# SwiGLU in quarters: 18 instead of 14 hidden tiles by seven products, two of the seven accumulated onto banks that were already read

## The chip, the cores and the metric

The kernel runs on one core of a Trainium2 chip. The metric is device time in microseconds (us), from the launch of the program to its end. The engines are named as the profile names them: PE is the tensor engine (PEld its weight loads), DVE the vector engine, ACT the scalar engine, POOL GpSimd, and SP the engine whose queue issues most of the DMAs. The profile sees the span from the first to the last instruction.

## What is computed

One decoder layer over 528 tokens (16 meta tokens and 512 main ones), with 1024 features: a half-weighted SwiGLU block, a mixing layer (attention and retention), and a second half-weighted SwiGLU block. The change touches the two SwiGLU blocks only:

```python
def swiglu(x, w_in, w_out):
    a, b = jnp.split(x @ w_in, 2, axis=-1)
    return (jax.nn.silu(a) * b) @ w_out

h = h + 0.5 * swiglu(rmsnorm(h, norm_ffn1), w_ffn1_in, w_ffn1_out)
...
h = h + 0.5 * swiglu(rmsnorm(h, norm_ffn2), w_ffn2_in, w_ffn2_out)
```

There are 2816 hidden features, that is 22 hidden tiles of 128 features, each with an `a` half and a `b` half. Everything is float32.

## The kernel before, in words

**Layout and precision.** Features lie on partitions, tokens on the free axis. Every dense product splits both float32 operands into a high and a low float32r part and takes three passes (high by high, high by low, low by high). ACT makes the high part by a copy, DVE the low part by a subtraction; the pair is the helper `split` (lines 104 to 106), so that each split is one ACT and one DVE instruction.

**A hidden tile as a whole.** `aj` and `bj` in the order `SEQ` (line 36) are the two halves of hidden tile j: eight chunks of 128 input features, three passes, each matmul over all tokens (two matmuls of 272 and 256 tokens in the first block, one of 512 in the second, which leaves the meta tokens out). `gated` then makes silu(a) times b.

**A hidden tile by seven products.** `ej` and `lj` compute both halves of tile j with seven products of quarters where a plain calculation has eight (a Strassen-like scheme). The quarters are the output halves, the contraction halves (chunks 0 to 3 and 4 to 7) and the token halves (t1, t2; 264 tokens each in the first block, 256 in the second). A product (`prod`) is four chunks by three passes, 12 matmuls. `early` (lines 387 to 404) has the first four products and `late` (lines 406 to 419) the last three. DVE adds and subtracts their results between the products. The scheme needs sums of the weights' quarters, made by `wsums` on DVE (lines 184 to 193: four additions of 512 columns per tile), and sums of the input's quarters, made by `usums` (lines 328 to 347), called at `u0` to `u3` for one pair of input chunks each; they are called `xa` and `xb` and can only be made once the norm's factor R is there. In the trace the products' tiles are `fq` in the first block and `sq` in the second, the whole halves `fpa`, `fpb`, `spa`, `spb`, and the output tiles (`pi`) `fpo`, `spo`.

**PSUM.** The products have four one-bank buffers (tag `pq`), the whole halves and output tiles two buffers of two banks (tag `ps`).

**Output tiles.** The hidden tiles are grouped in four parts of 6, 5, 6 and 5 (`PJ`). `pi` multiplies one of eight output tiles with part i, and DVE adds it onto the residual.

**The weights' stream.** SP loads 1 MB weight tiles ahead. A weight piece of up to 1024 columns is split into `wh` and `wl`, which have four buffers each. `weights()` (lines 219 to 224) hands out the next piece and first emits the splits of the pieces up to two further on. For a tile by seven products the pieces are `("A0","S1")`, `("A2","S0")`, `("A1","S2")` and `("A3",)`, where A0 to A3 are the tile's quarters as loaded (A2 is overwritten by a difference) and S0 to S2 sums of quarters; each name is a split of 512 columns of its own.

**Order.** PE's order is the one written in the code (`manual_schedule`). On DVE and ACT a scheduler places the instructions when the kernel is built: what is emitted earlier goes first among what is ready, and at run time each engine takes its instructions in the order so fixed. `gated` of tiles 0 to 3 is raised by 30 places.

Of the kernel before, what the change touches and what calls it, by code (L numbers as in the profile page):

```python
"""Hybrid decoder layer (FoX attention + retention between two half SwiGLU blocks), one core.

Everything is kept feature-major: features on partitions, tokens on the free axis.  The zero rows
that the reference puts before the meta tokens are masked everywhere, so the token axis here has the
16 meta tokens followed by the 512 main ones.  Dense products split both float32 operands exactly
into a float32r high and low part and take three passes (hh, hl, lh).  Most hidden tiles of the
SwiGLU blocks are computed by seven products of quarters (output halves x contraction halves x token
halves) instead of eight; the sums of quarters are float32 sums, split exactly like the other operands.
"""
# [11 lines left out]
ALU = mybir.AluOpType  # L21
# [10 lines left out]
# The order of a SwiGLU's work on the tensor engine, one token a piece or two of weights:  n0, n1: the  # L32
# first two hidden tiles; aj, bj: the halves of hidden tile j; ej, lj: a hidden tile by seven products of
# quarters, its first four and its last three; pi: the next output tile of the i-th part of the hidden
# tiles.  ui marks where the i-th chunk's sums of quarters are made.
SEQ = """n0 n1 a2 u0 b2 u1 a3 u2 b3 u3 a4 b4 e5 l5
          e6 p0 p0 l6 p0 e7 p0 p0 l7 p0 p0 p0
          e8 l8 e9 a10 l9 b10 e11 p1 l11 p1 p1 e12 p1 l12 p1 e13 p1 l13 p1 p1
          e14 a15 l14 b15 e16 l16 e17 p2 p2 l17 p2 e18 p2 p2 l18 p2 p2 p2
          e19 l19 e20 a21 l20 b21 p3 p3 p3 p3 p3 p3 p3 p3""".split()  # L40
# [12 lines left out]
# Tensor engine work (in units of its time) put between the steps of the attention: FOXFILL scales it,  # L53
# CREDIT is the number of the gates' tiles that go with a pair of heads.
# [10 lines left out]
def layer(tc, order, hT, wf1i, wf1o, wf2i, wf2o, wmix, wsq, vecs, cs, rmask, rvec, cmask, outT):  # L65
# [3 lines left out]
    with ExitStack() as es:  # L69
# [24 lines left out]
        def po_(a):  # L94
            """Where token 0 lies in a two-bank PSUM tile: no matmul's tokens cross the banks."""
            return PO if a == 0 else PM
# [15 lines left out]
        def weave(main, fill):  # L112
            """Emit main; what it yields is the tensor engine time to fill before it goes on."""
            have = 0.0
            for need in main:
                have -= need
                while have < 0:
                    got = next(fill, None)
                    if got is None:
                        have = 0.0  # L120
                        break
                    have += got

        # ---------------------------------------------------------------- the weights' stream
# [10 lines left out]
        def feed_ffn(seq, w_in, w_out):  # L135
            at_, nxt = {}, [0] * len(PJ)
            for tok in seq:
# [12 lines left out]
                if c in "nae":  # L150
# [3 lines left out]
                        "e": [("A0", "S1"), ("A2", "S0")], "l": [("A1", "S2"), ("A3",)]}[c]  # L154
                pieces.extend((at_[j], x, 1024) for x in cuts)
# [28 lines left out]
        def wsums(i):  # L184
            """Sums of a weight tile's quarters A11, A12, A21, A22: S1, S2, S4, and S3 in A21's place."""
# [9 lines left out]
        def ready(n):  # L195
            while at["p"] < min(n, len(pieces)):
# [11 lines left out]
                if i < 2:  # L208
                    for x in (0, 512):
                        split(wh[:, x:x + 512], wl[:, x:x + 512], raw[li][:, c + x:c + x + 512])  # L210
                        gained(2 * i + x // 512, gn1, u, 0, "n1")
                elif loads[li][2] == "S":
                    for x, src in enumerate(c):
                        src = (raw, sums)[src[0] == "S"][li][:, 512 * int(src[1]):512 * int(src[1]) + 512]
                        split(wh[:, 512 * x:512 * x + 512], wl[:, 512 * x:512 * x + 512], src)
                else:
                    split(wh[:, :w], wl[:, :w], raw[li][:, c:c + w])
# [8 lines left out]
        # ---------------------------------------------------------------- constants and first loads  # L226
# [41 lines left out]
        # ---------------------------------------------------------------- helpers  # L268
        def mm3(outs, w, x, nk, first=True, last=True):
            """outs = w^T x over nk chunks of 128, three float32r passes; outs: (psum, first token, end)."""  # L270
# [14 lines left out]
        def mm3s(out, w, x, start=True, stop=True):  # L285
            for i, (p, q) in enumerate(((w[0], x[0]), (w[0], x[1]), (w[1], x[0]))):
                nc.tensor.matmul(out, p, q, start=start and i == 0, stop=stop and i == 2)  # L287

        def gained(k, g, u, a, name):
            """u = h * gain, split into high and low parts."""  # L290
# [14 lines left out]
        def rstd(acc, R, outs, a, name, er=None):  # L305
            """R = rsqrt(mean square + eps) of every token, on all partitions."""
# [16 lines left out]
        # ---------------------------------------------------------------- SwiGLU  # L323
# [4 lines left out]
        def usums(c, gain, a, xs, name):  # L328
            """Sums of the quarters of h * gain * R (chunk halves x token halves), split: they pair
            tokens, which have one scale only when they are normed."""  # L330
# [18 lines left out]
        def ffn(seq, u, gain, a, pst, pq, norm, done, name):  # L349
# [5 lines left out]
            def prod(out, w, off, x, k0, ts, first, last):  # L355
                """out (+)= w^T x over four chunks: one of the seven products of quarters."""
                for k in range(4):
                    c = slice(off + 128 * k, off + 128 * k + 128)
                    mm3s(out, [z[:, c] for z in w], [z[k0 + k][:, ts] for z in x], first and k == 0, last and k == 3)
# [27 lines left out]
            def early(j):  # L387
                """The four products that the others' sums start from, and these sums."""
                b = [pq(f"{name}q{j}_{x}")[:, :nh] for x in range(4)]
                cu = ttile(f"{name}cu{j}")[:, :2 * nh]  # L390
                d = ttile(f"{name}d{j}")[:, :nh]
                bv = ttile(f"{name}b{j}")[:, :2 * nh]
                w = weights()
                prod(b[0], w, 0, u, 0, t1, True, True)
                nc.vector.tensor_tensor(cu[:, x1], b[0], R[:, t1], ALU.mult)
                prod(b[1], w, 512, xa, 0, x2, True, True)
                nc.vector.tensor_tensor(cu[:, x2], cu[:, x1], b[1], ALU.add)
                w = weights()
                prod(b[2], w, 512, xa, 0, x1, True, True)
                nc.vector.tensor_tensor(d, cu[:, x2], b[2], ALU.add)  # L400
                prod(b[3], w, 0, xb, 0, x1, True, True)
                nc.vector.tensor_tensor(bv[:, x1], cu[:, x2], b[3], ALU.add)
                nc.vector.tensor_tensor(bv[:, x2], d, b[3], ALU.add)
                return b, cu, d, bv

            def late(j, b, cu, d, bv):
                w = weights()
                prod(b[0], w, 0, u, 4, t1, True, True)
                prod(b[2], w, 512, u, 4, t2, True, True)
                prod(b[3], weights(), 0, xb, 0, x2, True, True)  # L410
                sv = ttile(f"{name}s{j}")[:, :2 * nh]
                nc.vector.tensor_tensor(sv[:, x1], b[0], R[:, t1], ALU.mult)
                nc.vector.tensor_tensor(sv[:, x2], b[2], R[:, t2], ALU.mult)
                nc.vector.tensor_tensor(bv[:, x1], bv[:, x1], b[3], ALU.add)
                nc.vector.tensor_tensor(sv[:, x1], sv[:, x1], cu[:, x1], ALU.add)
                nc.vector.tensor_tensor(sv[:, x2], sv[:, x2], d, ALU.add)
                nc.scalar.activation(sv, sv, AF.Silu)
                nc.vector.tensor_tensor(sv, sv, bv, ALU.mult)
# [3 lines left out]
            for tok in seq:  # L422
                c, j = tok[0], int(tok[1:])
                if tok == "n0":
# [3 lines left out]
                    # set aside: the tiles' banks are needed before R is there  # L428
# [25 lines left out]
                else:  # L454
# [5 lines left out]
                    # the last one in halves: the first is stored while the second is computed  # L460
# [6 lines left out]
        # ---------------------------------------------------------------- first SwiGLU  # L467
# [35 lines left out]
        # ---------------------------------------------------------------- mixing  # L503
# [8 lines left out]
        with tc.tile_pool(name="psM", bufs=1, space=PSUM, reuse_waits="tile") as pM:  # L512
# [9 lines left out]
            def proj(what, a, one=False):  # L522
                """One 128-wide tile of the combined projection of the unscaled u."""
# [9 lines left out]
            # ---- forget gate: running sum of the negated log sigmoid, every head a row in DRAM  # L533
# [36 lines left out]
            # ---- retention's projections  # L570
# [34 lines left out]
            # ---- forgetting attention  # L605
            y32 = [None] * KC
            last = {}
            with tc.tile_pool(name="fx", bufs=1, reuse_waits="tile") as fx:
# [11 lines left out]
                def qknorm(v, gain, a, name):  # L620
                    """Per-head RMS norm of a projected tile (64 features to a head), split: for each head of
                    a pair its keys' high and low parts one above the other, its queries' high part
                    twice, so that one pass of 128 rows carries both products with it."""
# [32 lines left out]
                def late(gen, fill):  # L656
                    """Run gen with its waits filled from fill; what is emitted is yielded on."""
# [12 lines left out]
                def values(p, v):  # L670
# [7 lines left out]
                    # a head's high and low parts side by side: one pass gives both products  # L678
# [542 lines left out]
```

## Time and profile before

| what | value |
|---|---|
| time, three runs | 1394.41, 1394.80 and 1395.88 us, median 1394.8 us |
| span of the profiled execution | 1392.1 us (its own time outside the span is not listed) |
| median less that span | 2.7 us |
| mean granted clock of PE | 0.999 of full speed |
| busy share PE, PEld, DVE, ACT | 99%, 89%, 72%, 48% |
| mean DMA traffic | 100 GB/s, 139.41 MB |

A share of busy time is a mean over stages with different limits; whether an engine sets the pace in one stage is read from that stage. Matmuls are pipelined: the listed duration of one is longer than the distance from its start to the start of the next. The same holds to a lesser degree on DVE and ACT, so that what an instruction costs in a full queue is the distance from start to start.

### The profile page before, as it was taken

Reading aid. Unit: us, or ns where it says so; the run is one execution under the profiler, and the core shown is the slowest. Engines: PE = TensorE matmul, PEld = TensorE weight load, DVE = VectorE, ACT = ScalarE, POOL = GpSimd, SP = SyncE. Lnnn points to the kernel's source line nnn. Section 1 sums busy time; section 2 is a strip of 40 time slices with the busy share of each in tenths; the row PEclk is TensorE's granted clock in tenths of the full one; section 3 lists DMA queues with packets and bytes.
Section 4 is the critical chain, followed back from the end, with each engine's and each line's share of the span. In section 5 each row is a group of like instructions: output and inputs, shape, how many; then the busy total and the mean of one; then the engine's idle time right before and its main releaser. Section 6 shows DMA issues by size and latency. Waiting matters only on the chain.

```text
span 1392.1 us, 22206 instructions
## 1 busy us (share of the span) xinstructions
PE 1376.5 (99%) x8871; PEld 1232.8 (89%) x8871; DVE 1007.9 (72%) x1948; ACT 666.7 (48%) x1131; POOL 52.6 (4%) x80
## 2 busy tenths in 40 slices
PE   8999999999999999999999999999999999999999
PEld 7999999999988788877878998888888889899897
DVE  7977877866687676677755866754666977788773
ACT  7433333333567577666754534453435433344331
POOL 0000000000013000010000000000100000000000
PEclk9999999999999999999999999999999999999999
DMA  7123222221513222222222112433521232223302
GB/s 276 46 106 110 79 101 106 84 103 64 201 61 109 92 84 71 90 92 84 92 84 91 61 61 71 139 124 136 191 108 57 80 127 82 99 93 121 109 21 97
DMA packets 27814, 139.41 MB, mean 100 GB/s; under 512 B 3632, under 2 KB 4016, under 8 KB 16576
## 3 DMA queue, kind: packets, MB, share of 16 engines
q1 hardware_dynamic: 24336, 127.31, 25.5%
q0 software_dynamic: 3232, 10.65, 2.6%
q8 instruction: 70, 1.15, 0.3%
q14 instruction: 32, 0.26, 0.1%
q10 hardware_dynamic: 144, 0.04, 0.0%
HBM read 129.56 MB, written 8.42 MB: 99 GB/s over the span
## 4 chain that ended last, share of the span: by engine, by line
PE 96%; DVE 2%; ACT 1%; DMA 0%; issue 0%; SPq 0%; DVEq 0%; ACTq 0%
PE fq L287 10%; PE sq L287 10%; PE fpo L277 9%; PE spo L277 9%; PE pg L277 6%; PE prv L277 3%; PE fpb L277 3%; PE pq L277 3%; PE fpa L277 3%; PE pv L277 3%; PE ow L277 3%; PE spa L277 3%; PE ob L277 3%; PE spb L277 3%; PE prg L277 3%; PE oa L277 3%
## 5 line engine op out<-in xcount | busy, mean ns | idle before, releaser
L105 ACT ACTIVATE wh<-w 128x512 fp32r<-128x512 f32 (+3 forms) x299 | 249.7, 835 | 465.6 <-PE fpo L277 69.1
L106 DVE TENSOR_TENSOR wl<-w,wh 128x512 fp32r<-128x512 f32 (+3 forms) x299 | 282.9, 946 | 68.3 <-ACT wh L105 66.0
L277 PE MATMUL fpo<-fgh,wh 128*128 128x272 f32 x352 | 71.4, 284 | 0.0
L277 PE MATMUL fpo<-fgl,wh 128*128 128x272 f32 x352 | 71.4, 284 | 0.0
L277 PE MATMUL fpo<-fgh,wl 128*128 128x272 f32 x352 | 71.2, 284 | 0.0
L277 PE MATMUL spo<-sgh,wl 128*128 128x512 f32 (+1 forms) x181 | 70.1, 387 | 0.0
L277 PE MATMUL spo<-sgh,wh 128*128 128x512 f32 (+1 forms) x181 | 70.0, 386 | 0.0
L277 PE MATMUL spo<-sgl,wh 128*128 128x512 f32 (+1 forms) x181 | 69.9, 386 | 0.0
L106 DVE TENSOR_TENSOR pl<-PT,ph 128x512 fp32r<-128x512 f32 (+4 forms) x80 | 34.6, 434 | 32.7 <-ACT ph L105 31.5
L106 DVE TENSOR_TENSOR wl<-ws,wh 128x512 fp32r<-128x512 f32 x84 | 57.6, 686 | 0.0
L277 PE MATMUL pg<-n2uh,wh 128*128 128x512 f32 x128 | 56.4, 440 | 0.0
L1116 DVE SCALAR_TENSOR_TENSOR hh<-spo,hh 128x512 f32<-128x512 f32 (+1 forms) x33 | 22.3, 675 | 44.9 <-PE spo L277 44.9
L793 ACT ACTIVATE P<-P,st 128x144 f32<-128x144 f32 (+1 forms) x64 | 36.5, 570 | 36.9 <-DVE st L789 36.1
L277 PEld LDWEIGHTS fpo<-fgh,wl 128*128 128x128 f32 x352 | 54.1, 189 | 0.0
L277 PEld LDWEIGHTS fpo<-fgh,wh 128*128 128x128 f32 x352 | 54.0, 188 | 0.0
L277 PEld LDWEIGHTS fpo<-fgl,wh 128*128 128x128 f32 x352 | 54.0, 188 | 0.0
L105 ACT ACTIVATE wh<-ws 128x512 fp32r<-128x512 f32 x84 | 51.7, 616 | 0.0
L277 PE MATMUL pg<-n2uh,wl 128*128 128x512 f32 x128 | 50.6, 395 | 0.0
L277 PE MATMUL pg<-n2ul,wh 128*128 128x512 f32 x128 | 50.4, 394 | 0.0
L492 DVE SCALAR_TENSOR_TENSOR h<-fpo,h 128x528 f32<-128x528 f32 x32 | 22.6, 707 | 37.8 <-PE fpo L277 37.8
L287 PE MATMUL fq<-n1ul,wh 128*128 128x264 f32 x168 | 48.0, 285 | 0.0
L287 PE MATMUL fq<-n1uh,wh 128*128 128x264 f32 x168 | 47.9, 285 | 0.0
(926 smaller groups left out, 4296.4 us busy)
## 6 DMA issues: line engine op xcount, KB each, us to landing
w<-in_wmix SPq DMA_DIRECT2D x32, 1024.0 KB, 4.9
w<-in_wf2i SPq DMA_DIRECT2D x22, 1024.0 KB, 4.9
w<-in_wf1i SPq DMA_DIRECT2D x21, 1024.0 KB, 4.9
w<-in_wsq SPq DMA_DIRECT2D x12, 1024.0 KB, 4.9
w<-in_wf1o SPq DMA_DIRECT2D x8, 768.0 KB, 4.2
w<-in_wf2o SPq DMA_DIRECT2D x8, 768.0 KB, 4.2
w<-in_wf1o SPq DMA_DIRECT2D x8, 640.0 KB, 3.9
w<-in_wf2o SPq DMA_DIRECT2D x8, 640.0 KB, 3.9
```

The source lines that it names most:

```text
L105: nc.scalar.activation(xh, src, AF.Copy)
L106: nc.vector.tensor_tensor(xl, src, f32(xh), ALU.subtract)
L277: nc.tensor.matmul(out, p[:, o:o + 128], q[:, a:b], start=first and k == 0 and i == 0, stop=last and k == nk - 1 and i == 2)
L287: nc.tensor.matmul(out, p, q, start=start and i == 0, stop=stop and i == 2)
L492: nc.vector.scalar_tensor_tensor(h[m][:, x:y], ps, 0.5, h[m][:, x:y], ALU.mult, ALU.add)
L793: last["exp"] = nc.scalar.activation(P[i][:, :w], P[i][:, :w], AF.Exp, scale=-1.0, bias=st[:, 2:3], accum_out=sm[:, 0:1])
L1116: nc.vector.scalar_tensor_tensor(h[m][:, x:y], ps, 0.5, h[m][:, x:y], ALU.mult, ALU.add)
```

## The change

It does five things, in both blocks:

1. Tiles 4, 10, 15 and 21 are no longer computed whole but by seven products. Tiles 0 to 3 stay whole; `SEQ` moves some of the output tiles to other places.
2. The products are taken in another order. In `early`, the third product adds onto the bank of the first (`onto`: the first matmul doesn't clear the bank) after DVE has read the first; in `late`, the third adds onto the bank of the first after DVE has read that. Each saves one DVE addition, so that a tile has nine DVE instructions on its products' results where it had eleven.
3. A tile takes three bank buffers in `early` and two in `late`, where it held four throughout.
4. The pieces of a tile by seven products are now neighbouring quarters: A0 with A1 (1024 columns), S0 with S1 (1024), A2 with A3 (1024) and S2 (512). Each is split by one ACT and one DVE instruction, where there were two for each piece of 1024.
5. `early` takes both of its pieces before its first product, and so does `late`.

```diff
-SEQ = """n0 n1 a2 u0 b2 u1 a3 u2 b3 u3 a4 b4 e5 l5
-          e6 p0 p0 l6 p0 e7 p0 p0 l7 p0 p0 p0
-          e8 l8 e9 a10 l9 b10 e11 p1 l11 p1 p1 e12 p1 l12 p1 e13 p1 l13 p1 p1
-          e14 a15 l14 b15 e16 l16 e17 p2 p2 l17 p2 e18 p2 p2 l18 p2 p2 p2
-          e19 l19 e20 a21 l20 b21 p3 p3 p3 p3 p3 p3 p3 p3""".split()
+SEQ = """n0 n1 a2 u0 b2 u1 a3 u2 b3 u3 e4 l4 e5 l5
+          e6 p0 l6 p0 e7 p0 p0 l7 p0 e8 p0 l8 p0 p0
+          e9 l9 e10 l10 e11 p1 l11 p1 e12 p1 l12 p1 p1 e13 p1 l13 p1 p1
+          e14 l14 e15 l15 e16 l16 e17 p2 l17 p2 p2 e18 p2 l18 p2 e19 p2 l19 p2 p2
+          e20 l20 e21 l21 p3 p3 p3 p3 p3 p3 p3 p3""".split()
...
-                        "e": [("A0", "S1"), ("A2", "S0")], "l": [("A1", "S2"), ("A3",)]}[c]
-                pieces.extend((at_[j], x, 1024) for x in cuts)
+                        "e": ["A0", "S0"], "l": ["A2", "S2"]}[c]
+                pieces.extend((at_[j], x, 512 if x == "S2" else 1024) for x in cuts)
...
-                    for x, src in enumerate(c):
-                        src = (raw, sums)[src[0] == "S"][li][:, 512 * int(src[1]):512 * int(src[1]) + 512]
-                        split(wh[:, 512 * x:512 * x + 512], wl[:, 512 * x:512 * x + 512], src)
+                    o = 512 * int(c[1])
+                    split(wh[:, :w], wl[:, :w], (raw, sums)[c[0] == "S"][li][:, o:o + w])
...
-                b = [pq(f"{name}q{j}_{x}")[:, :nh] for x in range(4)]
+                b = [pq(f"{name}q{j}_{x}")[:, :nh] for x in range(3)]
                 cu = ttile(f"{name}cu{j}")[:, :2 * nh]
                 d = ttile(f"{name}d{j}")[:, :nh]
+                sv = ttile(f"{name}s{j}")[:, :2 * nh]
+                w = weights()
+                v = weights()
+                prod(b[0], w, 0, u, 0, t1)
+                nc.vector.tensor_tensor(cu[:, x1], b[0], R[:, t1], ALU.mult)
+                prod(b[1], v, 512, xa, 0, x2)
+                nc.vector.tensor_tensor(cu[:, x2], cu[:, x1], b[1], ALU.add)
+                prod(b[0], w, 512, u, 4, t1, True)
+                nc.vector.tensor_tensor(sv[:, x1], b[0], R[:, t1], ALU.mult)
+                prod(b[2], v, 0, xa, 0, x1)
+                nc.vector.tensor_tensor(d, cu[:, x2], b[2], ALU.add)
+                return cu, d, sv
+
+            def late(j, cu, d, sv):
+                b = [pq(f"{name}r{j}_{x}")[:, :nh] for x in range(2)]
                 bv = ttile(f"{name}b{j}")[:, :2 * nh]
                 w = weights()
...
+                v = weights()
+                prod(b[0], w, 0, xb, 0, x1)
+                nc.vector.tensor_tensor(bv[:, x2], d, b[0], ALU.add)
+                prod(b[1], v, 0, u, 4, t2)
+                nc.vector.tensor_tensor(sv[:, x2], b[1], R[:, t2], ALU.mult)
                 nc.vector.tensor_tensor(sv[:, x2], sv[:, x2], d, ALU.add)
                 nc.scalar.activation(sv, sv, AF.Silu)
+                prod(b[0], w, 512, xb, 0, x2, True)
+                nc.vector.tensor_tensor(bv[:, x1], cu[:, x2], b[0], ALU.add)
                 nc.vector.tensor_tensor(sv, sv, bv, ALU.mult)
                 return sv
```

## Rows read from the trace of the kernel before

**Rows 1.** The page, parts 1 and 4: busy time, and the chain by engine.
```profile
PE 1376.5 (99%) x8871; PEld 1232.8 (89%) x8871; DVE 1007.9 (72%) x1948; ACT 666.7 (48%) x1131; POOL 52.6 (4%) x80
...
PE 96%; DVE 2%; ACT 1%; DMA 0%; issue 0%; SPq 0%; DVEq 0%; ACTq 0%
```
**Rows 2.** Waits of PE, longest in total first: total us, times, longest.
```profile
PE fpa L277 <- ACT n1uh L293: 6.1, 1, 6.1
PE pzt L542 <- DVE z L538: 1.2, 1, 1.2
```
**Rows 3.** Chain that ended last, in order of time: start us, us, what.
```profile
56.34 5.81 PE fpa L277 x48
...
67.97 16.07 PE fq L287 x132
...
1083.49 5.57 PE spa L277 x24
...
1094.64 15.58 PE sq L287 x132
```
**Rows 4.** Windows: stretch, length, busy us (instructions) of PE, PEld, DVE, ACT, POOL.
```profile
68.00:84.00 16.00, 16.00 (x133) 16.00 (x132) 15.10 (x30) 7.38 (x12) 0.00 (x0) 1.00 0.31 113
...
1095.00:1110.00 15.00, 15.00 (x129) 15.00 (x129) 14.75 (x29) 6.91 (x12) 0.00 (x0) 1.00 0.35 123
```
**Rows 5.** Timeline of DVE around tile 9's first product: start us, us, instruction.
```profile
143.39 1.23 DVE L106 TENSOR_TENSOR wl<-w,wh 128x1024 fp32r<-128x1024 f32 x1
144.53 0.42 DVE L414 TENSOR_TENSOR fb<-fb,fq 128x264 f32<-128x264 f32 x1
144.87 0.69 DVE L106 TENSOR_TENSOR wl<-w,wh 128x512 fp32r<-128x512 f32 x1
145.47 0.70 DVE L418 TENSOR_TENSOR fs<-fs,fb 128x528 f32<-128x528 f32 x1
146.09 0.43 DVE L395 TENSOR_TENSOR fcu<-fq,R 128x264 f32<-128x264 f32 x1
```
**Rows 6.** Timeline of DVE at the last input sums, first block.
```profile
60.61 0.71 DVE L106 TENSOR_TENSOR fxal<-fxa,fxah 128x528 fp32r<-128x528 f32 x1
61.23 0.69 DVE L106 TENSOR_TENSOR wl<-w,wh 128x512 fp32r<-128x512 f32 x1
61.83 0.71 DVE L106 TENSOR_TENSOR fxbl<-fxb,fxbh 128x528 fp32r<-128x528 f32 x1
```
**Rows 7.** Timeline of DVE at the last input sums, second block.
```profile
1088.22 0.70 DVE L106 TENSOR_TENSOR sxal<-sxa,sxah 128x512 fp32r<-128x512 f32 x1
1088.82 0.70 DVE L106 TENSOR_TENSOR wl<-ws,wh 128x512 fp32r<-128x512 f32 x1
```
**Rows 8.** Timeline of PE: last matmul of the first product, tiles 6 and 9.
```profile
79.38 0.29 PE L287 MATMUL fq<-n1uh,wl 128*128 128x264 f32 x1
...
144.97 0.29 PE L287 MATMUL fq<-n1uh,wl 128*128 128x264 f32 x1
```
**Rows 9.** Timeline of DVE around tile 6's first product.
```profile
79.62 0.95 DVE L106 TENSOR_TENSOR wl<-w,wh 128x768 fp32r<-128x768 f32 x1
80.49 0.70 DVE L106 TENSOR_TENSOR fgl<-fs,fgh 128x528 fp32r<-128x528 f32 x1
81.11 0.43 DVE L395 TENSOR_TENSOR fcu<-fq,R 128x264 f32<-128x264 f32 x1
```
**Rows 10.** Timeline of DVE after tile 5's fourth product; in brackets the wait.
```profile
73.85 0.43 DVE L402 TENSOR_TENSOR fb<-fcu,fq 128x264 f32<-128x264 f32 x1 [0.47 <-PE fq L287]
```
**Rows 11.** Instruction groups of DVE by form: busy us, mean ns.
```profile
L106 DVE TENSOR_TENSOR wl<-w,wh 128x1024 fp32r<-128x1024 f32 x119 | 146.5, 1231 | 39.8 <-ACT wh L105 38.5
L106 DVE TENSOR_TENSOR wl<-ws,wh 128x512 fp32r<-128x512 f32 x84 | 57.6, 686 | 0.0
L412 DVE TENSOR_TENSOR fs<-fq,R 128x264 f32<-128x264 f32 x14 | 6.0, 428 | 0.1
```

More of the change, by code (lines that the diff above doesn't have):

```diff
@@ L283, in views, with mm3s @@
             return [(ps[:, o + a:o + b], a, b) for a, b in ranges]
-        def mm3s(out, w, x, start=True, stop=True):
+        def mm3s(out, w, x, start=True, stop=True, onto=False):
             for i, (p, q) in enumerate(((w[0], x[0]), (w[0], x[1]), (w[1], x[0]))):
-                nc.tensor.matmul(out, p, q, start=start and i == 0, stop=stop and i == 2)
+                nc.tensor.matmul(out, p, q, start=start and i == 0, stop=stop and i == 2, skip_group_check=onto)
         def gained(k, g, u, a, name):
@@ L354, in ffn, with prod @@
             Rv = R[:, a:T]
-            def prod(out, w, off, x, k0, ts, first, last):
+            def prod(out, w, off, x, k0, ts, onto=False):
                 for k in range(4):
                     c = slice(off + 128 * k, off + 128 * k + 128)
-                    mm3s(out, [z[:, c] for z in w], [z[k0 + k][:, ts] for z in x], first and k == 0, last and k == 3)
+                    mm3s(out, [z[:, c] for z in w], [z[k0 + k][:, ts] for z in x], not onto and k == 0, k == 3, onto)
             g = {}
@@ L392, in early @@
                 bv = ttile(f"{name}b{j}")[:, :2 * nh]
                 w = weights()
[L394 to L415, printed above, removed]
+                v = weights()
```

## The prediction

> **What bounds the kernel now.** I read the page's busy shares and chain first: PE is busy 99% of the span and holds 96% of the chain that ended last [rows 1]. Then PE's waits: the longest are 6.1 us at the start and 1.2 us in the mixing stage, and none lies between two products [rows 2]. So in both SwiGLU blocks the time is the number of matmuls times their spacing, and a matmul less is time gained as long as PE goes on without a wait. Next I looked for the engine that is nearest to making PE wait. That is DVE: where two tiles by seven products follow each other without output tiles between them it is busy 15.10 of 16.00 us and 14.75 of 15.00 us [rows 4], though its mean is 72% [rows 1]. The last view is DVE's timeline, since what counts for the new order is how late DVE answers a product, and not only how busy it is.
>
> **What the change removes on PE.** A whole tile takes 67.97 - 56.34 = 11.63 us in the first block and 1094.64 - 1083.49 = 11.15 us in the second [rows 3]. A tile by seven products is 84 matmuls; the 132 of `early`, `late`, `early` take 16.07 and 15.58 us [rows 3], that is 121.7 and 118.0 ns each, so 10.23 and 9.91 us a tile. Four tiles in each block: 4 x 1.40 + 4 x 1.24 = 5.6 + 4.96 = 10.5 us less. This is sure as long as PE doesn't wait.
>
> **What it costs DVE.** From start to start in a full queue a 1024-wide split takes 144.53 - 143.39 = 1.14 us, a 264-wide sum 0.34, a 512-wide split 0.60, a 528-wide product 0.62 [rows 5]. A tile by seven products now takes 7 splits and 4 weight sums of 0.60, 10 sums of 0.34 and 2 of 0.62: 11.2 us. After the change it is 3 x 1.14 + 5 x 0.60 + 8 x 0.34 + 2 x 0.62 = 10.4 us. A whole tile took 2 x 1.14 + 4 x 0.62 = 4.8 us. So each of the 18 tiles is 0.9 us lighter, but each of the four converted ones 5.6 us heavier, and 10.4 us of DVE work stand against 10.23 us (9.91 in the second block) of PE work. Before, the whole tiles and output tiles gave DVE its rest; in the new order 4 and 5, then 9 and 10, then 14, 15 and 16, then 20 and 21 stand with nothing inside them. Over a block DVE has room; in these chains it has none.
>
> One rule of the Trainium skill would make this far worse. The 1024-wide split is listed with 1231 ns, the 512-wide with 686, the sum with 428 [rows 11]. The page "VectorE: DVE Perf Modes", section "The TRN2 errata — SBUF-src ops pay a fixed extra latency per instruction", gives a float32 addition of N columns (N+151)/0.96 ns, which is 691 ns for 512: the trace agrees, as the duration of one. Taken as what it costs in a queue, merging two splits would save 0.16 us, while the starts show 2 x 0.60 - 1.14 = 0.06 [rows 5]; a new tile would be 3 x 1.23 + 5 x 0.69 + 8 x 0.43 + 2 x 0.70 = 12.0 us. The starts decide for my sum; the other reading is a rival below.
>
> **Entering the first tile by seven products.** Before, tile 4 (11.63 us of PE) stood between the last input sums and tile 5. Now tile 4's second product needs `xa` of chunk 3 at once. DVE's work up to there is unchanged (norm, `gated` of tiles 0 to 3, input sums, the same two 1024-wide pieces), so I take `fxal` to end when it did: 60.61 + 0.71 = 61.32 [rows 6]. PE starts tile 4 at 56.34 [rows 3] and wants it at the 23rd matmul, 56.34 + 22 x 0.1217 = 59.02: a wait of 2.3 us. In the second block: 1088.22 + 0.70 = 1088.92 [rows 7] against 1083.49 + 22 x 0.118 = 1086.09: 2.8 us. Together 5.1 us. Low bound 0, if the scheduler puts these sums earlier; nothing in the diff raises them. `xb` (62.54 [rows 6]) is wanted only in `late`.
>
> Behind that, the third product waits until DVE has read the first bank, and the splits of pieces 3 and 4 of the tile are emitted before that read (both `weights()` now stand ahead of the products). One such split already got between the two input sums [rows 6]; as 1024 columns it is 1.14 us in front of the read. Low 0; high 1.14 + 0.60 + 0.62 = 2.4, if all of what is emitted earlier goes first. I take 1.14, twice: 2.3 us.
>
> **The new wait in every tile.** One product of 12 matmuls stands between the first product and the one that adds onto its bank. From the modelled end of the first product's last matmul to the start of the third product are 24 x 0.1217 - (11 x 0.1217 + 0.28) = 1.30 us. DVE must read within that. Before, nothing waited for this read until `late`. How late was it? In tile 9 the product ended at 144.97 + 0.29 = 145.26 [rows 8] and the read at 146.09 + 0.43 = 146.52 [rows 5]: 1.26 us. In tile 6: 79.38 + 0.29 = 79.67 [rows 8], 81.11 + 0.43 = 81.54 [rows 9]: 1.87 us, since a split for an output tile and the previous tile's `fgl` came first. Both stand right behind another tile's `late`, whose tail (last sum, product, `fgl`) fills DVE just then. In the new order 16 `early` do: 5, 6, 10, 11, 15, 16, 17 and 21 in each block. Ten of them (5, 10, 15, 16, 21) are followed by their own `late`: there the piece split at that moment is 1024 wide instead of 512, so 1.26 + 1.14 - 0.60 = 1.80, a wait of 0.50: 5.0 us. Low 0, if the split comes after the read; high 1.1 each, if a weight sum of 0.60 gets in as well. Six (6, 11, 17) have one output piece there: between 0 (as tile 9) and 1.87 - 1.30 = 0.57 (as tile 6); I take 0.3: 1.8 us. For the others, with output tiles in front, 0: DVE rests there. For the second such wait, in `late`, I take 0: the comparable read after the fourth product found DVE idle [rows 10]; high 0.5 at 18 adjacent pairs.
>
> **At no cost.** The weights' loads stay as many and as large. Five banks a tile rotate through four buffers and come round after at least 24 matmuls, 2.9 us, beyond the 1.87 above. ACT is busy 7.38 of 16.00 us in a chain [rows 4] and loses three instructions a tile. If that cover failed, one late piece would cost its split, 1.1 us.
>
> **Sum.** -10.5 + 5.1 + 2.3 + 5.0 + 1.8 = +3.7 us on the span of 1392.1 us. The median is 2.7 us above that span, which I keep: 1394.8 + 3.7 = 1398.5 us. I expect the waits to eat the matmuls saved, and a little more. 0.2% of the time, 2.8 us, is about what a measurement of this kernel can tell from no change.
>
> **Rivals.**
> - *DVE answers in time; only the entry is paid.* -10.5 + 5.1: 1389.4 us. It decides at the read's lateness: if it stays under 1.30 us behind a `late`, there is no wait. For it: tile 9's 1.26 [rows 5, 8], and two additions less per tile. Against it: tile 6's 1.87 [rows 9] and wider splits. Chance 0.30 (1387 to 1392).
> - *About even*: the entry in full, one in two of the waits behind `late`. -10.5 + 5.1 + 2.3 + 3.4 = +0.3: 1395.1 us. Chance 0.15.
> - *The matmuls come off in full*: the last input sums are placed before 59.02 too. 1384.3 us. Against it: DVE has no gap there in which they could move [rows 6]. Chance 0.04.
> - *Pieces and weight sums always first*: entry at its high, 1.1 us at each of the 16 places. -10.5 + 5.1 + 4.8 + 17.6 = +17.0: 1411.8 us. Chance 0.05.
> - *DVE paces the chains at its listed durations*: 12.0 - 10.23 = 1.75 us at the nine chained tiles of each block, 31.5 us: 1394.8 - 10.5 + 31.5 = 1415.8 us. The formula of the Trainium skill's page "VectorE: DVE Perf Modes" (the errata section) would lead here. Against it: DVE would need over 13 us a tile today (7 x 0.69 and 4 x 0.69, 10 x 0.43, 2 x 0.70), and PE doesn't wait. Chance 0.02.
>
> **How the numbers follow.** The forecast keeps 0.44, its own range 1394 to 1405 us. The range that holds 8 in 10 leaves out the full gain, the last two rivals and the edges of the rest: 1387 to 1408 us. Faster by over 0.2% (under 1392.0): 0.30 + 0.04 = 0.34. Within: 0.15 and a part of the forecast, 0.05. Slower: the rest, 0.46.
>
> **What would show it.** In the profile after: 672 `fq` and `sq` matmuls more and the four tiles' whole halves gone; PE's waits with `fq` waiting for `fxal` at tile 4 (about 2.3 us, 2.8 for `sq`), and for the reads `fcu` at tiles behind a `late` (0.3 to 0.6 us each). If PE's waits stay as short as now, the first rival is right. The forecast is wrong if the new DVE order puts the reads ahead of the wide splits, or if waits lie elsewhere: at the bank reuse, or at pieces that come late.

## The result, and the profile after

The changed kernel takes 1410.1 us (median; 1408.9 to 1411.1) beside 1394.6 us before: 1.0111 times the time of before, 95% interval 1.0096 to 1.0125. It is slower, as forecast, but by 15.5 us where 3.7 were forecast, and the time lies 2 us above the stated range. The span grew from 1392.1 to 1408.3 us.

Page of the changed kernel, parts 1 and 4:
```profile
PE 1376.6 (98%) x8967; PEld 1236.0 (88%) x8967; DVE 1035.4 (74%) x1904; ACT 672.7 (48%) x1063; POOL 51.4 (4%) x80
...
PE 84%; DVE 11%; ACT 2%; issue 2%; DMA 0%; SPq 0%; ACTq 0%; DVEq 0%
```
PE held 96% of the chain that ended last [rows 1] and now holds 84%; 11% have gone to DVE. So DVE sets the pace in places where it did not. The share does not say what that costs, since DVE's work there stands in the chain in place of PE's.

Waits of PE in the changed kernel, longest in total first (total us, times, longest):
```profile
PE fpa L276 <- ACT n1uh L292: 6.0, 1, 6.0
PE fq L286 <- DVE fcu L397: 3.2, 4, 2.2
PE sr L286 <- DVE sb L412: 3.0, 5, 0.9
PE sq L286 <- ACT sxah L105: 2.2, 1, 2.2
PE sq L286 <- DVE scu L397: 1.9, 4, 0.7
PE fr L286 <- DVE fb L412: 1.7, 4, 0.6
PE PV L850 <- DVE pl L106: 1.3, 2, 0.9
PE fq L286 <- ACT fxah L105: 1.3, 1, 1.3
```
The first and the seventh were there before. The others are new, and of two kinds: `fxah` and `sxah` are the last input sums, waited for by tile 4 (their low parts `fxal` and `sxal` follow further down the list with 0.5 and 0.8 us); `fcu`, `scu` (line 397) and `fb`, `sb` (line 412) are the reads after which a product may add onto its bank, in `early` and in `late`.

**The entry, tile 4.** Timeline of PE in the changed kernel (start us, us, instruction; in brackets the wait), first block, then second block:
```profile
57.94 0.28 PE L286 MATMUL fq<-n1uh,wh 128*128 128x264 f32 x1
...
61.98 0.39 PE L286 MATMUL fq<-fxah,wh 128*128 128x264 f32 x1 [1.32 <-ACT fxah L105]
62.89 0.39 PE L286 MATMUL fq<-fxal,wh 128*128 128x264 f32 x1 [0.52 <-DVE fxal L106]
...
65.59 0.59 PE L286 MATMUL fq<-n1uh,wh 128*128 128x264 f32 x1 [2.19 <-DVE fcu L397]
65.98 0.42 PE L286 MATMUL fq<-n1ul,wh 128*128 128x264 f32 x1
...
71.04 0.39 PE L286 MATMUL fr<-fxbh,wh 128*128 128x264 f32 x1
...
1090.52 0.28 PE L286 MATMUL sq<-n3uh,wh 128*128 128x256 f32 x1
...
1098.33 0.58 PE L286 MATMUL sq<-n3uh,wh 128*128 128x256 f32 x1 [0.74 <-DVE scu L397]
...
1102.96 0.28 PE L286 MATMUL sr<-sxbh,wh 128*128 128x256 f32 x1
```
From tile 4's first matmul to its third product stand 65.59 - 57.94 = 7.65 us where 24 matmuls at 0.1217 us take 2.92: 4.7 us lost; in the second block 7.81 - 2.83 = 5.0 us. By the starts of the matmuls these are, in the first block, 2.4 us for the input sums and 2.35 for the read, in the second 3.9 and 1.0. DVE's timeline shows what stood in front of the first block's read:
```profile
62.13 0.71 DVE L106 TENSOR_TENSOR fxal<-fxa,fxah 128x528 fp32r<-128x528 f32 x1
62.75 1.23 DVE L106 TENSOR_TENSOR wl<-w,wh 128x1024 fp32r<-128x1024 f32 x1
63.88 0.71 DVE L106 TENSOR_TENSOR fxbl<-fxb,fxbh 128x528 fp32r<-128x528 f32 x1
64.50 0.69 DVE L106 TENSOR_TENSOR wl<-ws,wh 128x512 fp32r<-128x512 f32 x1
65.10 0.43 DVE L397 TENSOR_TENSOR fcu<-fq,R 128x264 f32<-128x264 f32 x1
```
These are the last input sum that tile 4 needs at once, tile 4's third piece, the sum that it needs only in `late`, its fourth piece, and then the read. It is the high bound of the prediction's 0 to 2.4 us, line for line.

**The clock.** After this wait the matmuls of the third and fourth product lie 0.22 us apart instead of 0.12. Windows of the changed kernel (stretch, length, busy us and instructions of PE, PEld, DVE, ACT, POOL, then the granted clock):
```profile
60.00:65.00 5.00, 1.55 (x9) 0.93 (x7) 5.00 (x10) 1.93 (x3) 0.00 (x0) 0.94 0.00 0
65.00:70.00 5.00, 4.41 (x20) 4.41 (x21) 3.71 (x8) 1.06 (x1) 0.00 (x0) 0.50 0.61 210
...
74.00:78.00 4.00, 3.87 (x31) 3.65 (x31) 3.85 (x8) 2.29 (x3) 0.00 (x0) 1.00 0.16 27
```
PE worked 1.55 of 5 us, and in the next 5 us its clock is 0.50 of full speed, the lower of its two levels (1.2 instead of 2.4 GHz). The 24 matmuls from 65.59 to 71.04 took 5.45 us instead of 2.92: 2.5 us; in the second block 4.63 instead of 2.83: 1.8 us. The Trainium skill says the same of the cause (page "TensorE: Matmul & The Clock Gate", section "What's actually happening"): the lower level is the default, and activity releases it. The trace agrees, with the 0.50 above.

**The chains.** The chain that ended last, in order of time (start us, us, what), where tiles 9 to 11 and 14 to 17 begin and the output tile after them:
```profile
153.07 5.83 PE fq L286 x48
...
180.89 3.63 PE fpo L276 x30
...
234.82 5.84 PE fq L286 x48
...
273.43 4.38 PE fpo L276 x36
...
1261.48 5.70 PE sq L286 x48
...
1299.62 4.15 PE spo L276 x18
```
Tiles 9, 10 and `early` of 11 are 216 matmuls: 27.82 us instead of 26.3, so 1.5 lost. Tiles 14 to 16 and `early` of 17, 300 matmuls, lose 38.61 - 36.5 = 2.1 us in the first block and 38.14 - 35.4 = 2.7 in the second. With the rest of the first chain (1.8 and 2.0 us), tiles 9 to 11 of the second block (2.1) and tiles 20 and 21 (0.4 together) that is 12.7 us.

The sum, all from starts: -10.5 of matmuls, +9.7 at the entry, +4.3 of lower clock, +12.7 in the chains = +16.2 us, which is the difference of the spans. Two differences outside the changed parts nearly cancel in it: tile 4 of the first block starts 1.6 us later in this execution (57.94 against 56.34 [rows 3]), and from the end of that block's last output tile to tile 4 of the second block there are 1.5 us less (707.5 against 709.0).

**Why 12.7 us when the waits listed are less.** A wait in `late` of tile 10. PE, then DVE, in the changed kernel:
```profile
171.91 0.28 PE L286 MATMUL fr<-n1uh,wl 128*128 128x264 f32 x1
172.72 0.39 PE L286 MATMUL fr<-fxbh,wh 128*128 128x264 f32 x1 [0.53 <-DVE fb L412]
172.94 0.29 PE L286 MATMUL fr<-fxbl,wh 128*128 128x264 f32 x1
```
```profile
169.97 1.22 DVE L106 TENSOR_TENSOR wl<-w,wh 128x1024 fp32r<-128x1024 f32 x1
171.10 1.22 DVE L106 TENSOR_TENSOR wl<-ws,wh 128x1024 fp32r<-128x1024 f32 x1
172.24 0.43 DVE L412 TENSOR_TENSOR fb<-fd,fr 128x264 f32<-128x264 f32 x1
```
Listed are 0.53 us, counted from the modelled end of the matmul before. From start to start there are 0.81 us where 0.12 are usual, and 0.22 to the next: 0.79 us in all. A wait of this kind costs about 0.26 us more than is listed. Behind tile 4's `early`, the list has 6.9 us at 15 reads; with 0.26 each that is 10.8, and from start to start, with the delays too short to be listed, 12.2 of the 12.7 us. And in front of the read stand both pieces of the next tile, one after the other, which `late` takes before its first product.

**Where the reads cost nothing.** The 12.2 us lie otherwise than forecast. The third product of `late` lost 8.0 us, 0.4 to 1.2 us each at ten places (tiles 4, 5, 10, 15 and 16 of each block) and 0.6 in all at the others. The third product of `early` lost 0.6 us at each of tiles 6, 11 and 17, 3.8 us together in both blocks. At tiles 5, 10, 15, 16 and 21, for which the prediction has 0.50 us each, it lost 0.4 us in all ten together. Tile 10, PE (the first product's last matmul, the third product's first), then DVE:
```profile
164.50 0.29 PE L286 MATMUL fq<-n1uh,wl 128*128 128x264 f32 x1
...
166.08 0.37 PE L286 MATMUL fq<-n1uh,wh 128*128 128x264 f32 x1
```
```profile
164.37 0.69 DVE L106 TENSOR_TENSOR wl<-ws,wh 128x512 fp32r<-128x512 f32 x1
164.97 0.70 DVE L419 TENSOR_TENSOR fs<-fs,fb 128x528 f32<-128x528 f32 x1
165.59 0.43 DVE L397 TENSOR_TENSOR fcu<-fq,R 128x264 f32<-128x264 f32 x1
```
The split in front of this read is S2, 512 columns wide, and not one of 1024. The read ends 1.23 us after the product (166.02 against 164.79), as it did at tile 9 before (1.26), and so within the 1.30 us of cover.

### The profile page after: what moved, and what is told of

Same layout as the page of the kernel before. It is cut to its first block, busy times and chain, and to the rows that moved or that the text cites. A ratio compares the mean times of both kernels' runs of the same rounds, so it can differ in the third digit from the quotient of the medians.

```text
span 1408.3 us, 22179 instructions
## 1 busy us (share of the span) xinstructions
PE 1376.6 (98%) x8967; PEld 1236.0 (88%) x8967; DVE 1035.4 (74%) x1904; ACT 672.7 (48%) x1063; POOL 51.4 (4%) x80
## 4 chain that ended last, share of the span: by engine, by line
PE 84%; DVE 11%; ACT 2%; issue 2%; DMA 0%; SPq 0%; ACTq 0%; DVEq 0%
PE fpo L276 9%; PE spo L276 9%; PE pg L276 6%; PE sq L286 6%; PE fq L286 6%; PE fr L286 5%; PE sr L286 4%; PE prv L276 3%; PE pq L276 3%; PE ow L276 3%; PE ob L276 3%; PE prg L276 3%; PE pv L276 3%; PE oa L276 3%; PE pk L276 3%; DVE wl L106 2%
## 5 line engine op out<-in xcount | busy, mean ns | idle before, releaser
L105 ACT ACTIVATE wh<-w 128x1024 fp32r<-128x1024 f32 (+3 forms) x243 | 238.5, 981 | 381.2 <-PE fpo L276 55.7
L106 DVE TENSOR_TENSOR wl<-w,wh 128x1024 fp32r<-128x1024 f32 (+3 forms) x243 | 274.9, 1131 | 60.9 <-ACT wh L105 57.6
L105 ACT ACTIVATE wh<-ws 128x1024 fp32r<-128x1024 f32 x72 | 60.8, 845 | 89.4 <-PE fq L286 26.2
L106 DVE TENSOR_TENSOR wl<-ws,wh 128x1024 fp32r<-128x1024 f32 x72 | 68.8, 956 | 4.1 <-ACT wh L105 2.8
L794 ACT ACTIVATE P<-P,st 128x144 f32<-128x144 f32 (+1 forms) x64 | 36.5, 570 | 35.6 <-DVE st L790 34.5
L105 ACT ACTIVATE ph<-PT 128x512 fp32r<-128x512 f32 (+4 forms) x80 | 31.3, 393 | 31.7 <-PE PT L830 23.9
L286 PE MATMUL fq<-n1uh,wh 128*128 128x264 f32 x144 | 42.2, 293 | 3.2 <-DVE fcu L397 3.2
L286 PE MATMUL sr<-sxbh,wh 128*128 128x256 f32 x144 | 41.1, 285 | 3.0 <-DVE sb L412 3.0
```

What stands on the lines that cost most here:

```text
L105: nc.scalar.activation(xh, src, AF.Copy)
L106: nc.vector.tensor_tensor(xl, src, f32(xh), ALU.subtract)
L794: last["exp"] = nc.scalar.activation(P[i][:, :w], P[i][:, :w], AF.Exp, scale=-1.0, bias=st[:, 2:3], accum_out=sm[:, 0:1])
```

## The experiments

Each time is a median, with the difference to the kernel before on the same chip beside it, since those medians lie between 1393.8 and 1394.6 us.

| kernel | us | to before, us | ratio (95% interval) |
|---|---|---|---|
| the change | 1410.1 | +15.5 | 1.0111 (1.0096 to 1.0125) |
| 17 tiles, tile 4 whole | 1397.7 | +3.7 | 1.0021 (1.0012 to 1.0030) |
| 14 tiles, new products | 1404.2 | +10.2 | 1.0067 (1.0050 to 1.0084) |
| 18 tiles, old products | 1394.8 | +0.8 | 1.0006 (0.9996 to 1.0015) |
| 18 tiles, wait filled | 1405.0 | +11.0 | 1.0080 (1.0065 to 1.0095) |
| 18 tiles, narrow splits | 1409.0 | +15.3 | 1.0109 (1.0092 to 1.0125) |
| 18 tiles, own banks | 1394.7 | +0.9 | 1.0005 (0.9995 to 1.0014) |
| 18 tiles, exchange | 1402.3 | +8.5 | 1.0059 (1.0044 to 1.0074) |
| 17 tiles, exchange, read raised | 1387.1 | -6.7 | 0.9951 (0.9936 to 0.9966) |
| 18 tiles, second piece later | 1400.6 | +6.6 | 1.0050 (1.0033 to 1.0066) |
| 18 tiles, both reads raised | 1395.9 | +1.9 | 1.0011 (1.0002 to 1.0021) |
| 18 tiles, exchange, read raised | 1395.6 | +1.6 | 1.0012 (1.0003 to 1.0021) |
| 17 tiles, old products | 1386.6 | -7.5 | 0.9944 (0.9929 to 0.9959) |

**Tile 4 whole again.**
```diff
-SEQ = """n0 n1 a2 u0 b2 u1 a3 u2 b3 u3 e4 l4 e5 l5
+SEQ = """n0 n1 a2 u0 b2 u1 a3 u2 b3 u3 a4 b4 e5 l5
```


> The changed kernel with tile 4 computed whole again (17 tiles by seven products in each block). My theory: the first tile by seven products behind the input sums costs what it loses up to its third product (4.7 us in the first block, 5.0 in the second) and what the lower clock after that wait adds (2.7 and 1.8 us), 14.2 us in all; the two conversions undone give 2.6 us back to the tensor engine. So 1410.1 - 14.2 + 2.6 = 1398.5 us, and the clock's mean is 0.999 again. Rival, the load of DVE as such: the wait only moves on to tile 5, and the time stays within 3 us of 1410.

Measured: 1397.7 us, mean clock 1.000. One tile of 18 in each block costs 15.5 - 3.7 = 11.8 us net. The waits for the input sums are gone, while those for the reads stay. The rival falls.

**New products, old order.** The changed kernel with the `SEQ` of before.


> The new products, banks and pieces with the order of before (14 tiles by seven products). My theory: the reads that the accumulating products wait for come too late behind a neighbour's late part and in late itself, so the tensor engine waits at the four places of each block where an early follows a late directly; 0.5 to 0.9 us each, 1398 to 1402 us. Rival: the new products only make DVE lighter and cost nothing at 14 tiles: 1394.6 us, no new wait of the tensor engine.

Measured: 1404.2 us, more than the theory's range. The waits are at seven places in each block and not at four: an `early` behind a whole tile waits too. In all 4.7 us are listed, with 0.26 at each of 14 places 8.3 of the 10.2 us. From start to start the products of this kernel lose 9.2 us in all; the remaining 1 us I can't place. DVE's timeline at tile 6 of this kernel:
```profile
82.35 0.95 DVE L106 TENSOR_TENSOR wl<-w,wh 128x768 fp32r<-128x768 f32 x1
83.21 0.70 DVE L106 TENSOR_TENSOR fgl<-fs,fgh 128x528 fp32r<-128x528 f32 x1
83.83 0.42 DVE L397 TENSOR_TENSOR fcu<-fq,R 128x264 f32<-128x264 f32 x1
```
It is the picture of [rows 9]: the split for an output tile, the previous tile's `fgl`, the read. Before, nothing waited for that read; now PE does. So the new products, as ordered here, lose against the old ones even where DVE has its whole tiles to rest on.

**Old products, new order.** The kernel before with the `SEQ` of the change.


> The products, banks and pieces of before with the new order (18 tiles). My theory: without a product that waits for a read, the entry waits only for the input sums (2.3 and 2.8 us, with perhaps 2 to 4 us of lower clock), and DVE's 11.2 us a tile against 10.2 stops the chains later and less: 1394.6 - 10.5 + 5.1 + 4 + 5 = 1398 us, below the changed kernel by 10 us or more. Rival, DVE's load decides: as DVE has 0.9 us more a tile here, it is at 1410 us or above.

Measured: 1394.8 us, no change from before. With 14.7 us less than the change at the same 18 tiles, and more work on DVE, the rival falls. The entry's waits are there still (2.5 us listed for `sxah`, 1.3 for `fxah`), and at tile 6, still behind the entry, stands a wait that 17 tiles of old products don't have:
```profile
PE sq L287 <- DVE ss L412: 1.1, 1, 1.1
PE fq L287 <- DVE fs L412: 0.9, 1, 0.9
```
There the second product waits until DVE has read a bank of tile 5. By starts, the two entries lose 10.4 us in all: 6.0 for the input sums, 2.6 for tile 6's wait, about 1.5 at the lower clock in the second block, and 0.3 in shorter delays. That eats the 10.5 us that the matmuls save.

**The wait filled.** Spare matmuls onto a free bank, at tile 4 only:
```diff
+            def spare(n):
+                z = pst(f"{name}z{n}")
+                for _ in range(n):
+                    nc.tensor.matmul(z[:, 0:nh], u[0][0][:, a:a + 128], u[0][0][:, t1], start=True, stop=True)
...
+                p1, p2 = ((13, 21) if name == "f" else (25, 12)) if j == 4 else (0, 0)
```


> The changed kernel with 13 and 21 spare matmuls (25 and 12 in the second block) where tile 4 waits for the input sums and for the first read; their results are not used. My theory: the clock falls to its lower level because the tensor engine stands still there, and with work in the gap it stays up: the 2.7 and 1.8 us that the lower clock costs are saved, 1410.1 - 4.5 = 1405.6 us. Rival, the time lost there is waiting alone: the spare matmuls fit into the gap at best, 1410 us, or add to it.

Measured: 1405.0 us, 4.5 us less to before than the change, for 71 matmuls more. The window of this kernel that answers to the one at 0.50 above:
```profile
65.00:70.00 5.00, 5.00 (x44) 5.00 (x43) 5.00 (x9) 2.12 (x2) 0.00 (x0) 1.00 0.38 159
```
The clock stays at 1.00, and by starts tile 4 loses as much up to its third product as before (4.8 and 5.1 us): only the slow matmuls behind it are gone. The lower clock is a cost of its own, and it is PE's standing still in the wait that brings it.

**Narrow splits.** The pieces stay, each quarter is split by itself:
```diff
-                    split(wh[:, :w], wl[:, :w], (raw, sums)[c[0] == "S"][li][:, o:o + w])
+                    src = (raw, sums)[c[0] == "S"][li]
+                    for x in range(0, w, 512):
+                        split(wh[:, x:x + 512], wl[:, x:x + 512], src[:, o + x:o + x + 512])
```


> The changed kernel with every weight quarter of a tile by seven products split by itself (512 columns), the accumulating products kept. My theory: the accumulating products make the tensor engine wait for DVE's reads, and what stands in front of a read is a wide split and the neighbour's store; narrow splits shorten the waits by up to 0.54 us at each of about 26 places but don't remove them: 1398 to 1403 us. Rival, the width of the splits is the whole cause: 1395 us or less. Rival, the width plays no part: 1408 to 1412 us.

Measured: 1409.0 us. My theory falls here: the time does not go with the width (+15.3 against +15.5 us). The waits do move: those of the six `early` behind tile 4 are no longer listed (2.2 us before), those in `late` grew from 4.7 to 6.7 us. DVE's timeline in this kernel at the place shown above, `late` of tile 10:
```profile
169.33 1.29 DVE L106 TENSOR_TENSOR wl<-w,wh 128x512 fp32r<-128x512 f32 x2
170.54 1.29 DVE L106 TENSOR_TENSOR wl<-ws,wh 128x512 fp32r<-128x512 f32 x2
171.74 0.42 DVE L414 TENSOR_TENSOR fb<-fd,fr 128x264 f32<-128x264 f32 x1
```
Four narrow splits stand where two wide ones stood, and the read comes after all of them. Not the length of one instruction delays it, but all that is put ahead of it.

**Own banks.** The third product of `early` and of `late` in a bank of its own, with the addition on DVE back:
```diff
-                prod(b[0], w, 512, u, 4, t1, True)
-                nc.vector.tensor_tensor(sv[:, x1], b[0], R[:, t1], ALU.mult)
+                prod(b[3], w, 512, u, 4, t1)
+                nc.vector.tensor_tensor(sv[:, x1], b[3], R[:, t1], ALU.mult)
+                nc.vector.tensor_tensor(sv[:, x1], sv[:, x1], cu[:, x1], ALU.add)
```
(and likewise in `late`).


> The changed kernel with the third product of early and of late in banks of their own and one more addition on DVE for each, the wide splits kept. My theory: without the two waits for a read only the entry's wait for the input sums is left, as with the old products: 1393 to 1397 us, though the wide splits and both additions are in. Rival, the wide splits delay DVE whatever waits for it: 1402 us or more.

Measured: 1394.7 us. The two waits for a read, with the lower clock that they bring in the first block (there it stays at 1.00 here), cost 15.5 - 0.9 = 14.6 us; the wide splits and the two additions more cost nothing that can be told from the old products' +0.8. In PE's waits the reads `fcu` and `scu` are gone. What is left is mostly the entry, and behind it 1.7 us for banks (`fb`, `sb`), as with the old products:
```profile
PE sq L286 <- ACT sxah L105: 2.2, 1, 2.2
...
PE fq L286 <- ACT fxah L105: 1.3, 1, 1.3
```

**Exchange.** Third and fourth product of `early` in the other order, 24 matmuls of cover instead of 12:
```diff
-                prod(b[0], w, 512, u, 4, t1, True)
-                nc.vector.tensor_tensor(sv[:, x1], b[0], R[:, t1], ALU.mult)
                 prod(b[2], v, 0, xa, 0, x1)
                 nc.vector.tensor_tensor(d, cu[:, x2], b[2], ALU.add)
+                prod(b[0], w, 512, u, 4, t1, True)
+                nc.vector.tensor_tensor(sv[:, x1], b[0], R[:, t1], ALU.mult)
```


> The changed kernel with the third and fourth product of early exchanged, so that 24 matmuls instead of 12 stand between the first product and the one that adds onto its bank. My theory: all waits for the first read go (about 5.4 us in the chains), the entry loses about 3 us of its wait and part of its time at the lower clock; the waits in late stay: 1397 to 1401 us. Rival, DVE's load in the chains sets their time: the waits move to late and the time stays above 1406 us.

Measured: 1402.3 us, just above the range. Of the waits for the first read one is left, of 0.7 us; those in `late` grew from 4.7 to 7.5 us listed. So part of what is won in `early` is lost in `late`, as the rival had it, but not all.

**17 tiles, exchange, late's read raised.** The two edits above, and:
```diff
-                nc.vector.tensor_tensor(bv[:, x2], d, b[0], ALU.add)
+                with tc.high_priority(offset=60):
+                    nc.vector.tensor_tensor(bv[:, x2], d, b[0], ALU.add)
```


> 17 tiles (tile 4 whole), the third and fourth product of early exchanged, and late's first read raised by 60 places in the scheduler's order. My theory: the waits for the first read (5.4 us) go, and most of those in late (5.1 us); what is left of the matmuls saved, 7.9 us, is nearly all gain: 1387 to 1391 us. Rival, DVE's load in the chains: 1394 us or more.

Measured: 1387.1 us, faster than both kernels; 7.9 us of matmuls taken off give 6.7. The chain in order of time at tiles 9 and 10 of this kernel:
```profile
155.88 5.83 PE fq L286 x48
161.72 4.39 PE fr L286 x36
166.11 5.83 PE fq L286 x48
171.94 3.63 PE fpo L276 x30
```
PE goes through without a break, though DVE has 10.4 us of work a tile against 10.2 there.

**Second piece later.** `v = weights()` behind the first product's read, in `early` and in `late`.


> The changed kernel with the second piece of early and of late taken only after the first product's read, so that one split less is emitted ahead of the read. My theory: it is the splits emitted ahead of a read that make it late, in late above all, where both pieces of the next tile stand in front: about 0.5 to 1 us less at each of 10 to 16 places, 1397 to 1403 us. Rival, DVE has too much work in the chains whatever its order: the waits move elsewhere and the time stays above 1407 us.

Measured: 1400.6 us, 8.9 us less to before than the change. One piece less ahead of each read is worth more than half of what the reads cost.

**Both reads raised.** Lines 397 and 412 of the change inside `high_priority(offset=60)`.


> The changed kernel with both reads that an accumulating product waits for raised by 60 places in the scheduler's order, nothing else. My theory: the chains' 12.4 us shrink to 3 or less, and the entry's wait by 2 to 3 us with part of the lower clock: 1392 to 1398 us. Rival, DVE's load: 1405 us or more.

Measured: 1395.9 us. Only DVE's and ACT's order differs from the change, the products still add onto banks already read, and 13.6 of the 14.6 us are gone. The reads' lateness is a matter of order.

**18 tiles, exchange, late's read raised.**


> 18 tiles with the third and fourth product of early exchanged and late's read raised by 60 places. My theory: of the time with the exchange alone, 1402.3 us, the waits in late go (7.5 us listed, some 10 us with the start of the pipeline): 1391 to 1395 us. The input sums' wait at tile 4 stays, so it is 3 to 7 us slower than with 17 tiles (1387.1). Rival: with the reads in time 18 tiles beat 17, under 1386 us.

Measured: 1395.6 us, a little above the range, and 8.3 us more to before than with 17 tiles. My 3 to 7 us for tile 4 were too few: the lower clock comes on top of its wait here too (mean clock 0.996), and tile 6's first read is waited for (0.8 and 1.0 us listed).

**17 tiles, old products.**


> The products, banks and pieces of before with the new order but tile 4 whole (17 tiles). My theory: the old products wait for no read, and the entry is covered by the whole tile; of the 7.9 us of matmuls saved most is gain: 1386 to 1390 us. Rival: DVE's 11.2 us a tile stop the tensor engine in the chains without whole tiles: 1393 us or more.

Measured: 1386.6 us, the lowest of all, with 7.5 of 7.9 us gained. 18 against 17 tiles is 8.3 us again. The 17 tiles with the new products in time (-6.7 us) can't be told from it, as the intervals overlap. So the order of the tiles alone gives all that was gained; that the new products add anything is not shown.

## Why the prediction was right and wrong

- *Matmuls taken off, 10.5 us.* Right: with the entry covered and no read waited for, 17 tiles give 7.5 of the 7.9 us that three conversions a block are worth.
- *The entry's wait for the input sums, 5.1 us.* Right in place and cause, and not far off in size: 2.4 us in the first block (forecast 2.3) and 3.9 in the second (2.8), where `sxal` ends 6.2 us after the tile's start and not 5.4. But the wait is not the whole price of tile 4: without the reads it costs 8.3 us net, and with the 2.6 us of matmuls that its conversion saves 10.9 gross (old products, and again with the exchange). What the prediction lacked is the lower clock and what comes late at tile 6.
- *The step that failed: where the new wait falls, 6.8 us in `early` and 0 in `late`.* The mechanism was right: a product that adds onto a bank waits for DVE's read. The term taken as 0 was the largest: in `late` 8.0 us were lost. The row that I leaned on [rows 10] showed a read that found DVE idle, with nothing ahead of it; in the new `late` both pieces of the next tile stand there. The 5.0 us at ten `early` reads were 0.4: I put a 1024-wide split in front of them, and the trace has the 512-wide S2. The 1.8 us at the six others were 3.8; of each, about 0.26 us is what counting from the modelled end of a matmul leaves out. Together 12.2 us instead of 6.8.
- *The read at the entry, taken as 1.14 us "twice".* It was mis-sized in one block. In the first it came to 2.35 us, near its high bound of 2.4: all that was emitted earlier stood in front. In the second it came to 1.0. Up to the third product 9.7 us were lost instead of 7.4.
- *What no step had: the granted clock.* Behind the entry's waits, with few matmuls between them, PE fell to its lower level: 4.3 us by the starts and 4.5 us by the filled wait.
- *DVE's load in the chains.* The forecast kept the starts (10.4 us a tile) against the listed durations (12.0 us), and rightly: the raised read at the same load goes through without a break. The rule of the page "VectorE: DVE Perf Modes" of the Trainium skill (section "The TRN2 errata — SBUF-src ops pay a fixed extra latency per instruction") holds for one instruction's duration (691 ns for 512 columns by the page, 686 listed); as a price in a queue, no run here bears it out (0.60 us from start to start [rows 5]).
- *"Wider splits" as an argument for a late read.* It fell: narrow splits move the waits and leave the time.
- *The sum, by differences of times.* Matmuls -10.5, tile 4's entry without the reads +10.9 (forecast 5.1, for the input sums alone), the reads +14.6 (forecast 2.3 + 6.8): +15.0 of the 15.5 us.
- *The range.* It ended at 1408 us. That the case "pieces and weight sums always first" gives 1411.8 us, near the measured time, is luck: its 17.6 us stand on the sixteen `early` reads, which lost 4.2, and it has neither `late` nor the clock.

Open: 1 us of the 10.2 with 14 tiles and the new products, and 0.5 us of the 12.7 in the chains.

## What to carry to other kernels

A product that adds onto a bank already read saves an addition on the vector engine and puts a round trip into the tensor engine's order. It can pay only where the read is sure to come within the cover, and what decides that is all that is emitted ahead of the read, not how wide each of those instructions is. Here, with the reads in time, it brought nothing that can be told from the old products (1387.1 and 1386.6 us). When an engine's work is shifted, count what is placed in front of the waited-for instruction, take the whole of it, and then either raise that instruction or put more products between. And when a tensor engine that never stood still gets a wait of several us, price the clock after it as well.

## What was not expected of the hardware

The lower clock followed waits that were interrupted: in the first block 1.32, 0.52 and 2.19 us with a few matmuls in between, and then 0.50 of full speed for about 6 us. With the old products the first block's wait for the same sums (1.30 and 0.67 us) left the clock at 1.00, while behind the second block's (2.49 and 0.49 us) it fell to a mean of 0.79 over 8 us: two waits of the same kind, one with the lower clock and one without. It also differs between executions of one kernel: of the ten of the kernel with own banks, the one with a mean clock of 1.000 took 1391.6 us, the three at 0.996 took 1394.5 to 1395.6. And a listed wait of 0.53 us cost 0.79.
